# Five small changes of order in a fused encoder layer on one core: both ends, two recurrence heads, the attention's scores, and the first two loads of the output projection

## The chip, the cores and the metric

The kernel runs on one core of a Trainium2 chip. The metric is the device time of one execution in microseconds (us), as the median of several runs. Lower is better. Engine names are those of the profile: PE is TensorE (matmuls), PEld its weight loads, DVE is VectorE, ACT is ScalarE, POOL is GpSimd, SP is SyncE. SP issues nearly all loads; ACT and SP issue the stores.

## The reference

One encoder layer for 512 tokens of width 1024 in float32, cut to what matters:

```python
h = rms_norm(x, norm1_g)
proj = h @ w_in                       # pool, attention, recurrence inputs and three gates
y_pool = pool_mixer(u, pool_w, pool_scale)           # centred means over 2, 4, 8, 16 tokens
y_attn = diff_attention(aq, ak, av, lam, gain)       # 4 heads, two softmaxes each, ALiBi
y_rec  = hgrn2_mixer(rq, rf, rb, ri, rg, lb, gain)   # 4 heads, forward and backward scans
merged = g0 * (y_pool @ w_up_pool) + g1 * (y_attn @ w_up_attn) + g2 * (y_rec @ w_up_rec)
x = x + merged @ w_out
h2 = rms_norm(x, norm2_g)
gu = h2 @ w_ffn_in
x = x + (silu(gu[:, :2816]) * gu[:, 2816:]) @ w_ffn_out
return rms_norm(x, final_norm_g)
```

## The kernel before

**Matmuls.** Large products run as three float32r matmuls: both factors are split into a high part (a cast on ACT) and a low part (a subtraction on DVE), and hi·hi, lo·hi and hi·lo are summed in PSUM. For a weight these are `whi` (L185) and `wlo` (L186), for the normalised input `hT_hi` (L496) and `hT_lo` (L500). Small products of the recurrence and all transposes are plain float32 matmuls of 128x128.

**Weights.** A `Chunk` is one DMA of a weight (1 MB, or 512 KB) into a raw tile. By default the tile comes from the ring `wraw` of two buffers; a chunk with `where` takes it from a named pool (`LAST[where]`), which must have been opened. A `Part` is a piece of a chunk that is split into `whi` and `wlo`; three splits are held ahead. `Jobs.pump` emits loads in the order of the chunks: at most two live chunks of `wraw`, and a chunk with `where` as soon as its pool is there. Each engine works its own queue in order, so an instruction that waits holds all behind it on its engine. The orders of ACT, DVE and SP are set by a scheduler from its own simulated times (`issue_after` binds some of them), that of PE by the program.

**Order.** The layer runs in stages, and in each one several streams are woven together by `Pipe`: a planner with its own clock `t`, which each matmul advances by a fixed cost. A stream that yields `("w", c)` comes on again after `c` us of that clock; one that yields `("e", name, c)` comes on `c` us after the event `name`. The matmuls of `jobs.stream` fill what is between. PE's order of instructions is that of emission.

- At the start (L541 to about L600) four blocks of 128 rows of x are loaded. The gain row of the first norm is spread over 128 partitions by PE (`rc<-ident,g1c`) and copied to `g1b` in two halves by DVE (L577). `norm_rows` squares a block on ACT (L477), takes the reciprocal root on POOL (`ms` L148, then the power, L142), and multiplies on DVE in two halves (`hrow`, L483). `rows_T` transposes on PE (L98), and `hT_hi`, `hT_lo` follow. `probe` is filler for PE.
- `rec_scan(h)` is the stream of one recurrence head. After the event `V` it computes the states between blocks (`rc<-v_rec,kT`: two directions of three products, then `st` copies on ACT, L948, and the running sums on DVE, L951), waits 1.6 on the planner's clock and issues the outputs (`rc<-pt,v_rec` and `rc<-kq,st`). `kq,kc` are the products within a block, `pt` (L924) is their masked result. All share three PSUM banks named `rc`.
- `att_head(h)` is that of an attention head; it starts 6.0 after the event `AF{h}`, which stands behind the projection of keys. That evacuation makes k as hi parts and `l` as lo parts, the last of them by a copy on ACT (L1025). Scores are `rc<-k,q` and `rc<-l,q`. At a head's end the sums of squares go through PE (`tp<-fixed,sqo`), small DVE steps, a power on POOL (`rso`) and back through PE (`tp<-ident,rso`).
- The output projection: `quarter_parts(w_out[0], 0, 512, "wx")` gives two chunks of 256 columns, q0 and q1; `row_parts` gives two chunks for the other 512 columns, the row chunks, 1 MB each, whose splits go to a pool of their own. Beside them SP loads x again (2 MB) and `g2b`. Before the first quarter the last `up_job`s finish the merged tiles: for the tiles 4 to 7, DVE multiplies and adds (L758 to L762), ACT casts the hi part (L765, `y_arena<-gate`), DVE subtracts for the lo part (L766). `out_quarter_job` runs three blocks over k-tiles 0 to 5 first and then k-tiles 6 and 7.
- At the end `seven_job` finishes block after block of the final sum. `out_add` (L1410) adds PSUM to x; `out_sums` squares on ACT (L1417) and multiplies by the final gain on DVE (L1419); `out_rstd` sums on DVE and takes the power on POOL; `out_store(b)` scales 512 columns on ACT and 512 on DVE (L1441, L1443) and stores each half (256 KB) from ACT's and SP's queue. `behind` keeps what it holds after given instructions.

Of the kernel before, what the change touches and what calls it, by code (L numbers as in the profile page):

```python
# [14 lines left out]
AF = mybir.ActivationFunctionType  # L15
# [7 lines left out]
KT = D // P  # L23
# [15 lines left out]
class Pipe:  # L39
# [8 lines left out]
    def mark(self, name):  # L48
        self.events[name] = self.t
# [27 lines left out]
def encoder_kernel(ctx: ExitStack, tc: tile.TileContext, x, norm1_g, w_in, pool_w, pool_scale,  # L77
# [3 lines left out]
    nc = tc.nc  # L81
# [187 lines left out]
    @contextmanager  # L269
    def behind(after):  # L270

        with ExitStack() as st:
            for i in after:
                st.enter_context(tc.issue_after(i))
            yield
# [165 lines left out]
    def quarter_parts(w, c0, n, where=None, skip=0):  # L441

        v = w.rearrange("(kt p) c -> p kt c", p=P)
        for c in range(0, n, 256):
            ch = Chunk(v[:, :, c0 + c:c0 + c + 256], KT, 256, where if c == 0 else None)
            yield slice(c, c + 256), [Part(ch, lambda raw, j=j: raw[:, j:j + 4, :], 4, 256, None, skip)
                                       for j in (0, 4)]

# [78 lines left out]
    g_b = xg.tile([P, D], F32, name="g1b")  # L527
# [8 lines left out]
    for b in range(NB):  # L536
# [6 lines left out]
        if b >= 1:  # L543
            c = OFF[("rq", "rf", "rb")[b - 1]]
# [23 lines left out]
    gt = bank("tp")  # L568
# [4 lines left out]
    for half in range(2):  # L573
        gt = bank("rc", (P, 4, P))
        for j in range(4):
            transpose(gt[:, j, :], g_cols[:, half * 4 + j:half * 4 + j + 1].to_broadcast([P, P]), ident)
        nc.vector.tensor_copy(out=g_b[:, half * 512:half * 512 + 512], in_=gt.rearrange("p a b -> p (a b)"))  # L577

    probe = xg.tile([P, 1024], F32R, name="probe")
    nc.scalar.copy(out=probe, in_=ident.rearrange("p (o c) -> p o c", o=1).to_broadcast([P, 8, P]))  # L580
# [7 lines left out]
    first = []  # L588
# [10 lines left out]
    for b in range(2):  # L599
        where = ("tp", "rc")[b]  # L600
# [37 lines left out]
    for i in range(3):  # L638
        for n, _ in enumerate(cols_mm(ps0[i], first[i], hT, KT, 0, 0, 256, i == 0)):
            if (i, n) in ((1, 5), (2, 5)):  # L640
                b = 1 + i
# [227 lines left out]
    def rec_scan(h):  # L869
# [3 lines left out]
        kq, f, q = fronts[h]  # L873
# [26 lines left out]
        while n < P:  # L900
# [17 lines left out]
            a = strided(tot, toff, [[tstep, 2], [2, nb2]])  # L918
            c = strided(tot, toff + 1, [[tstep, 2], [2, nb2]])
# [9 lines left out]
        for d in range(2):  # L929
            ps = bank("rc", (P, NB, P))  # L930
            for j in range(3):
                b = j + d
# [1 line left out]
            nc.scalar.copy(out=kT[:, 3 * d:3 * d + 3, :], in_=ps[:, 0:3, :])  # L934
        mark(f"S{h}")
        yield ("e", "V", 0.8)
        yield ("w", 1.0)
        st = rh.tile([P, 6, P], F32, name="st", bufs=2)
        vs = [v_rec[:, b, h * P:(h + 1) * P] for b in range(NB)]
        for d in range(2):  # L940
# [4 lines left out]
            for prev, j in zip((None,) + order, order):  # L945
                own = st[:, 3 * d + j, :]
                if prev is None:
# [2 lines left out]
                total = strided(pyr, toff + d * S + j + d, [[1, 1]])  # L950
                nc.vector.scalar_tensor_tensor(out=own, in0=st[:, 3 * d + prev, :], scalar=total, in1=ps[:, j, :],  # L951
                                               op0=ALU.mult, op1=ALU.add)
        yield ("w", 1.6)
        ps = bank("rc")
        for b in range(NB):
            o = ps[:, b * P:(b + 1) * P]
# [77 lines left out]
    def att_head(h):  # L1034
        if h:
            yield ("e", f"QK{h - 1}", 0.0)
        if h > 1:
            yield ("e", f"AN{h - 2}", 0.0)
        yield ("e", f"AF{h}", 6.0)
        t = att.pop(h)  # L1040
        at, (vh, vl), aT, y_attn = ATT["at"], ATT["v"], ATT["aT"], ATT["y"]
        strip = ATT["strip"].tile([P, 896], F32, name="strip")
        nc.sync.dma_start(out=strip, in_=c_dist[h])
        zz = at.tile([P, NB, 2], F32, name="zz")
        rr = at.tile([P, NB], F32, name="rr")
        probs = {}

        def scores(i):
            bs = slice(i * P, (i + 1) * P)
            mx = small.tile([P, 2], F32, name="mx")  # L1050
            ex = []
            for c in range(2):
                ps = bank("rc")
                mm(ps, t[f"q{c}"][:, bs], t[f"k{c}"], True, False)
                mm(ps, t[f"q{c}"][:, bs], t[f"l{c}"], False, True)
                s = at.tile([P, S], F32, name=f"s{c}")

                nc.vector.tensor_tensor_reduce(out=s, in0=strip[:, 384 - P * i:896 - P * i], in1=ps, scale=1.0,  # L1058
                                               scalar=3.0e38, op0=ALU.add, op1=ALU.min, accum_out=mx[:, c:c + 1])
                nc.scalar.activation(out=s, in_=s, func=AF.Exp, scale=-1.0, bias=mx[:, c:c + 1],  # L1060
                                     accum_out=zz[:, i, c:c + 1])
                ex.append(s)

            co = small.tile([P, 2], F32, name="co")
            zn, co = co[:, 0:1], co[:, 1:2]
            nc.gpsimd.tensor_tensor(out=zn, in0=zz[:, i, 0:1], in1=nlam, op=ALU.mult)
            nc.gpsimd.tensor_tensor(out=co, in0=zz[:, i, 1:2], in1=minus1, op=ALU.pow)
            nc.gpsimd.tensor_tensor(out=co, in0=co, in1=zn, op=ALU.mult)
            nc.vector.scalar_tensor_tensor(out=ex[0], in0=ex[1], scalar=co, in1=ex[0], op0=ALU.mult, op1=ALU.add)
            probs[i] = ex[0]  # L1070

        def turn(i):
            bs = slice(i * P, (i + 1) * P)
            p = probs.pop(i)
            pt = bank("tp", (P, NB, P))
            for k in range(NB):
                transpose(pt[:, k, :], p[:, k * P:(k + 1) * P], ident)
            nc.scalar.copy(out=aT[0][:, :, bs], in_=pt)
            nc.vector.tensor_tensor(out=aT[1][:, :, bs], in0=pt, in1=aT[0][:, :, bs].bitcast(F32), op=ALU.subtract)

        scores(0)
        for i in range(NB):
            yield ("w", 1.6 + (0.7 if i == 0 else 0.0))
            if i + 1 < NB:
                scores(i + 1)
            else:
                mark(f"QK{h}")
            yield ("w", 2.4 + (1.0 if i + h == 0 else 0.0))
            if h and i == 0:
                yield ("e", f"PV{h - 1}", 0.0)  # L1090
            turn(i)
        mark(f"T{h}")
        nc.vector.reciprocal(out=rr, in_=zz[:, :, 0])
        yield ("e", "VA", 1.5)
        yield ("w", 1.5)
        ps = bank("rc")
        es = slice(h * P, (h + 1) * P)
        terms = [(vh, aT[0]), (vl, aT[0]), (vh, aT[1])]
        for i, (a, r) in enumerate(terms):
            for k in range(NB):  # L1100
                mm(ps, a[:, k, es], r[:, k, :], i == 0 and k == 0, i == 2 and k == NB - 1)
            yield
        mark(f"PV{h}")
        og, rbp = yield from head_norm(ps, at, gain_a, rr, 1)
        mark(f"AN{h}")
        nc.vector.tensor_tensor(out=og, in0=og, in1=rbp, op=ALU.mult)
        nc.scalar.copy(out=y_attn[0][:, h, :], in_=og)
        nc.vector.tensor_tensor(out=y_attn[1][:, h, :], in0=og, in1=y_attn[0][:, h, :].bitcast(F32),
                                op=ALU.subtract)
# [302 lines left out]
    def out_sums(b, c0, w, col, out_=None):  # L1412

        x = out_cols(b, c0, w)
        junk = FF["t"].tile([P, S], F32, name="silu")
        col = 4 * b + col
        sq = nc.scalar.activation(out=junk[:, 0:w], in_=x, func=AF.Square, scale=D ** -0.5,  # L1417
                                  accum_out=FF["stats"][:, col:col + 1]).ins
        nc.vector.tensor_tensor(out=x if out_ is None else out_, in0=x, in1=FF["g"][:, c0:c0 + w], op=ALU.mult)  # L1419
        return sq  # L1420
# [5 lines left out]
    def out_rstd(b, n):  # L1426

        st = [FF["stats"][:, 4 * b + i:4 * b + i + 1] for i in range(n)]
        ms = small.tile([P, 1], F32, name="ss2")
        if n == 2:  # L1430
            on_dve = nc.vector.tensor_tensor(out=ms, in0=st[0], in1=st[1], op=ALU.add).ins
        else:
            on_dve = nc.vector.scalar_tensor_tensor(out=ms, in0=st[1], scalar=st[0], in1=st[2],
                                                    op0=ALU.add, op1=ALU.add).ins
        rstd = small.tile([P, 1], F32, name="rstd")
        pow_mhalf(rstd, ms)
        return rstd, on_dve

    def out_store(b, rstd, src=None):
        a, c = out_cols(b, 512, 512), out_cols(b, 0, 512)  # L1440
        nc.scalar.activation(out=a, in_=a, func=AF.Copy, scale=rstd)  # L1441
        nc.scalar.dma_start(out=outb[b][:, 512:], in_=a)
        nc.vector.tensor_scalar(out=c, in0=c if src is None else src, scalar1=rstd, scalar2=None, op0=ALU.mult)  # L1443
        nc.sync.dma_start(out=outb[b][:, 0:512], in_=c)
# [157 lines left out]
    def seven_job():  # L1602
# [76 lines left out]
        late, _ = out_rstd(2, 2)  # L1679
        yield  # L1680
        own = bank("tp")
        src = FF["t"].tile([P, S], F32, name="u")
        first, second = slice(0, 256), slice(256, 512)
        sv_product(x[1][:, first], 7, 1, False, True, first)
        out_add(3, 256, x[1][:, second], ALU.subtract)
        out_add(3, 0, x[1][:, first], ALU.subtract)
        out_sums(3, 0, 256, 1, src[:, first])
        sv_product(own[:, second], 7, 1, True, True, second)
        out_add(3, 256, own[:, second], ALU.subtract)
        sq = out_sums(3, 256, 256, 2, src[:, second])  # L1690
        rstd, on_dve = out_rstd(3, 3)
        with behind((sq, on_dve)):
            out_store(2, late)
        out_store(3, rstd, src)
        yield

    for i, (j, _) in enumerate(PLAIN):
        ch = Chunk(wo[:, j:j + 2, :], 2, D)
# [136 lines left out]
```

## Time and profile before

| | us |
|---|---|
| median of 3 runs | 881.21 (880.99 to 881.6) |
| profiled execution | 880.92 |
| its span | 879.0 |
| PE busy | 866.3 (99%) |
| DVE busy | 660.8 (75%) |
| ACT busy | 448.9 (51%) |
| POOL busy | 37.8 (4%) |

The mean granted clock of TensorE is 0.998 of full speed, and the DMA engines moved 87.54 MB, at a mean of 100 GB/s. In a timeline each line is a start, a duration, an engine with its line, the operation with its output and inputs, and a count; in brackets stand the idle time before it and what ended it. "x3" lines are runs of like instructions. PE's matmuls overlap, so the duration of one is longer than the distance to the next.

### The profile page before, as it was taken

What the parts mean: (1) busy time and instruction counts of PE and PEld (TensorE: products, weight loads), DVE (VectorE), ACT (ScalarE), POOL (GpSimd) and SP (SyncE); (2) the same over time, 40 slices, a digit from 0 to 9 for tenths busy, and PEclk for the clock granted to TensorE, in tenths of its full rate; (3) what the DMA queues carried; (4) which work ended last, traced back from release to release, by engine and by line L of the source; (5) the groups of instructions that cost most, each with busy time, mean ns of one, the idle gap of its engine ahead of it and who ended that gap; (6) DMA issues with size and microseconds to landing.
All of it is one profiled execution on the core that took longest, in us unless ns stands there. A gap on an engine that the chain in (4) does not pass through costs nothing.

```text
span 879.0 us, 14111 instructions
## 1 busy us (share of the span) xinstructions
PE 866.3 (99%) x5713; PEld 786.4 (89%) x5713; DVE 660.8 (75%) x978; ACT 448.9 (51%) x718; POOL 37.8 (4%) x83
## 2 busy tenths in 40 slices
PE   8999999999999999999999999999999999999996
PEld 7989988888997888899999898999999999988885
DVE  6788655854757787987876645997888888847996
ACT  6544333525747764563355335755655655533563
POOL 2000000000112230000000001000000000000001
PEclk9999999999999999999999999999999999999999
DMA  8330113124133131343331770253433433355002
GB/s 244 97 120 25 50 48 96 48 73 138 45 96 94 52 104 48 97 134 107 96 97 48 263 192 1 54 139 106 135 97 98 137 102 98 120 192 191 1 1 97
DMA packets 115694, 87.54 MB, mean 100 GB/s; under 512 B 3862, under 2 KB 104748, under 8 KB 115628
## 3 DMA queue, kind: packets, MB, share of 16 engines
q1 hardware_dynamic: 115036, 85.57, 32.2%
q8 instruction: 45, 0.74, 0.4%
q10 hardware_dynamic: 592, 1.05, 0.3%
q14 instruction: 21, 0.17, 0.1%
HBM read 84.52 MB, written 2.10 MB: 99 GB/s over the span
## 4 chain that ended last, share of the span: by engine, by line
PE 86%; issue 7%; DVE 3%; DMA 2%; ACT 1%; POOL 1%; POOLq 0%; DVEq 0%; ACTq 0%
PE mm L90 56%; PE rc L90 26%; PE tp L90 2%; PE tp L98 2%; DMA raw<-in_w_out_dram 1%; DVE wlo L186 1%; DVE hrow L483 1%; DMA raw<-in_w_in_dram 0%; ACT whi L185 0%; DVE hT_lo L500 0%; PE rc L98 0%; ACT s L1060 0%; POOL rso L142 0%; DVE g1b L577 0%; ACT l L1025 0%
## 5 line engine op out<-in xcount | busy, mean ns | idle before, releaser
L185 ACT CAST whi<-raw 128x1024 fp32r<-128x1024 f32 (+1 forms) x134 | 127.6, 958 | 141.5 <-PE mm L90 90.7
L186 DVE TENSOR_TENSOR wlo<-raw,whi 128x1024 fp32r<-128x1024 f32 (+1 forms) x134 | 147.5, 1106 | 51.2 <-ACT whi L185 35.4
L90 PE MATMUL mm<-hT_hi,whi 128*128 128x512 f32 (+1 forms) x344 | 82.4, 371 | 0.0
L90 PE MATMUL mm<-hT_hi,wlo 128*128 128x512 f32 (+1 forms) x344 | 81.4, 370 | 0.2 <-DVE wlo L186 0.2
L90 PE MATMUL mm<-hT_lo,whi 128*128 128x512 f32 (+1 forms) x344 | 81.1, 369 | 0.0
L304 DVE TENSOR_TENSOR slo<-sums,shi 128x1024 fp32r<-128x1024 f32 x58 | 70.6, 1218 | 0.3 <-ACT shi L302 0.3
L90 PEld LDWEIGHTS mm<-hT_hi,whi 128*128 128x128 f32 x344 | 59.0, 189 | 9.8 <-ACT hT_hi L496 0.4
L90 PEld LDWEIGHTS mm<-hT_lo,whi 128*128 128x128 f32 x344 | 59.1, 189 | 9.5
L90 PEld LDWEIGHTS mm<-hT_hi,wlo 128*128 128x128 f32 x344 | 58.7, 189 | 9.6 <-DVE wlo L186 0.4
L302 ACT CAST shi<-sums 128x1024 fp32r<-128x1024 f32 x58 | 61.0, 1052 | 4.6 <-DVE sums L266 3.7
L263 DVE TENSOR_TENSOR sums<-raw 128x1024 f32<-128x1024 f32 x29 | 35.4, 1219 | 1.5 <-DMA raw<-in_w_in_dram 1.5
L90 PE MATMUL mm<-y_arena,whi 128*128 128x512 f32 x128 | 32.5, 394 | 0.0
L90 PE MATMUL mm<-whi,y_arena 128*128 128x256 f32 (+1 forms) x192 | 31.9, 316 | 0.2 <-ACT whi L185 0.2
L916 DVE TENSOR_TENSOR kq<-kq,pyr 128x256 f32<-128x256 f32 x48 | 18.2, 421 | 18.1 <-PE rc L90 18.0
L90 PE MATMUL rc<-kq,kc 128*128 128x128 f32 x224 | 31.6, 285 | 0.0
L90 PEld LDWEIGHTS rc<-kq,kc 128*128 128x128 f32 x224 | 30.1, 191 | 1.5
L90 PEld LDWEIGHTS mm<-whi,y_arena 128*128 128x128 f32 x192 | 27.4, 188 | 3.2 <-ACT whi L185 0.8
L885 ACT COPY kc<-kq 128x512 f32<-128x512 f32 x28 | 18.6, 666 | 20.4 <-PE rc L90 12.7
L1060 ACT ACTIVATE s<-s,mx 128x512 f32<-128x512 f32 x32 | 23.1, 721 | 10.9 <-DVE mx L1058 10.7
L90 PEld LDWEIGHTS mm<-y_arena,whi 128*128 128x128 f32 x128 | 23.8, 188 | 5.0
L1350 DVE TENSOR_TENSOR g<-mm,g 128x256 f32<-128x256 f32 x21 | 8.9, 424 | 23.7 <-PE mm L90 23.7
L90 PE MATMUL mm<-fhi,slo 128*128 128x256 f32 x168 | 26.1, 278 | 0.6 <-DVE slo L304 0.5
(386 smaller groups left out, 2045.7 us busy)
## 6 DMA issues: line engine op xcount, KB each, us to landing
raw<-in_w_in_dram SPq DMA_DIRECT2D x44, 512.0 KB, 4.1
raw<-in_w_ffn_in_dram SPq DMA_DIRECT2D x44, 512.0 KB, 5.3
raw<-in_w_in_dram SPq DMA_DIRECT2D x8, 1024.0 KB, 5.2
raw<-in_w_ffn_out_dram SPq DMA_DIRECT2D x7, 1024.0 KB, 4.9
raw<-in_w_out_dram SPq DMA_DIRECT2D x4, 1024.0 KB, 11.1
xin<-in_x_dram SPq DMA_DIRECT2D x4, 512.0 KB, 4.6
raw<-in_w_up_rec_dram SPq DMA_DIRECT2D x2, 1024.0 KB, 6.6
raw<-in_w_up_pool_dram SPq DMA_DIRECT2D x2, 1024.0 KB, 5.1
```

Source lines behind the costliest of these rows:

```text
L90: i = nc.tensor.matmul(out_, lhsT=lhsT, rhs=rhs, start=start, stop=stop, skip_group_check=chain)
L98: tc.keep_in_program_order(nc.tensor.transpose(out_, in_, idn))
L185: nc.scalar.copy(out=hi, in_=view)
L186: LAST["wlo"] = nc.vector.tensor_tensor(out=lo, in0=view, in1=hi.bitcast(F32), op=ALU.subtract).ins
L263: nc.vector.tensor_tensor(out=strided(sums, 0, [[2 * half, 2], [1, half]]), in0=strided(self.raw, 0, [[3 * half, 2], [1, half]]), in1=stri ...
L302: nc.scalar.copy(out=hi, in_=view)
L304: on_dve = nc.vector.tensor_tensor(out=lo, in0=view, in1=hi.bitcast(F32), op=ALU.subtract).ins
L483: on_dve = nc.vector.scalar_tensor_tensor(out=h[:, cs], in0=src[:, cs], scalar=rstd, in1=g_b[:, cs], op0=ALU.mult, op1=ALU.mult).ins
L885: nc.scalar.copy(out=strided(kc, 0, [[2 * n, S // (2 * n)], [n, 2], [1, n]]), in_=strided(kq, 2 * S, [[2 * n, S // (2 * n)], [S + n, 2], [ ...
L916: nc.vector.tensor_tensor(out=xv, in0=xv, in1=tv, op=ALU.mult)
L1060: nc.scalar.activation(out=s, in_=s, func=AF.Exp, scale=-1.0, bias=mx[:, c:c + 1], accum_out=zz[:, i, c:c + 1])
L1350: on_dve = nc.vector.tensor_tensor(out=c["g"], in0=c["x"], in1=c["g"], op=ALU.add).ins
```

## The change

There are five edits. (1) Of the two quarter chunks of w_out, the second now goes to the pool `wx`, the first to the ring `wraw`. (2) The second half of the gain row is copied by ACT. (3) Head 1's states come 4.5 and not 1.0 after `V` plus 0.8, and the outputs of heads 0 and 1 come 2.4 after the states and not 1.6. (4) Heads 2 and 3 of the attention start 7.0 after `AF`. (5) The store of block 2 is emitted behind the sums of the first half of block 3, and no longer behind the last sums.

```diff
-            ch = Chunk(v[:, :, c0 + c:c0 + c + 256], KT, 256, where if c == 0 else None)
+            ch = Chunk(v[:, :, c0 + c:c0 + c + 256], KT, 256, where if c else None)
...
-        nc.vector.tensor_copy(out=g_b[:, half * 512:half * 512 + 512], in_=gt.rearrange("p a b -> p (a b)"))
+        (nc.scalar.copy if half else nc.vector.tensor_copy)(
+            out=g_b[:, half * 512:half * 512 + 512], in_=gt.rearrange("p a b -> p (a b)"))
...
-        yield ("w", 1.0)
+        yield ("w", 4.5 if h == 1 else 1.0)
...
-        yield ("w", 1.6)
+        yield ("w", 2.4 if h < 2 else 1.6)
...
-        yield ("e", f"AF{h}", 6.0)
+        yield ("e", f"AF{h}", 7.0 if h > 1 else 6.0)
...
-        out_sums(3, 0, 256, 1, src[:, first])
+        with behind((out_sums(3, 0, 256, 1, src[:, first]),)):
+            out_store(2, late)
...
-        sq = out_sums(3, 256, 256, 2, src[:, second])
-        rstd, on_dve = out_rstd(3, 3)
-        with behind((sq, on_dve)):
-            out_store(2, late)
-        out_store(3, rstd, src)
+        out_sums(3, 256, 256, 2, src[:, second])
+        out_store(3, out_rstd(3, 3)[0], src)
```

In the changed kernel the lines from L578 to L1686 have numbers one higher, those behind L1694 one lower.

PE in the recurrence, heads 0 and 1, before. `rc<-v_rec,kT` are the state products, `rc<-pt,v_rec` and `rc<-kq,st` the outputs, `mm<-hT_hi,whi` a projection:

```order
L90 MATMUL mm<-hT_hi,whi 128x512 x6
L90 MATMUL rc<-kq,kc 128x128 x4
L90 MATMUL rc<-v_rec,kT 128x128 x12
L90 MATMUL mm<-hT_hi,whi 128x512 x2
L90 MATMUL rc<-pt,v_rec 128x128
L90 MATMUL rc<-kq,st 128x128
L90 MATMUL rc<-pt,v_rec 128x128
L90 MATMUL rc<-kq,st 128x128 x2
```

The same place now:

```order
L90 MATMUL mm<-hT_hi,whi 128x512 x6
L90 MATMUL rc<-kq,kc 128x128 x4
L90 MATMUL rc<-v_rec,kT 128x128 x6
L90 MATMUL mm<-hT_hi,whi 128x512 x2
L90 MATMUL mm<-hT_lo,whi 128x512 x6
L90 MATMUL rc<-kq,kc 128x128 x4
L90 MATMUL rc<-pt,v_rec 128x128
L90 MATMUL rc<-kq,st 128x128
```

Head 1's six state products have gone from here; they stand behind the outputs of head 0, and eight projection matmuls and four `kq,kc` stand between head 0's states and its outputs.

ACT around the output projection, before. `whi<-raw` are the casts of weights, `y_arena<-gate` those of the merged tiles 4, 5, 6 and 7:

```order
L716 ACTIVATE gate<-mm 128x256
L765 CAST y_arena<-gate 128x512 x2
L185 CAST whi<-raw 128x1024 x2
L765 CAST y_arena<-gate 128x512
L185 CAST whi<-raw 128x1024
L765 CAST y_arena<-gate 128x512
L185 CAST whi<-raw 128x1024 x8
```

The same place now:

```order
L185 CAST whi<-raw 128x1024
L717 ACTIVATE gate<-mm 128x256
L766 CAST y_arena<-gate 128x512
L185 CAST whi<-raw 128x1024
L766 CAST y_arena<-gate 128x512 x2
L185 CAST whi<-raw 128x1024 x3
L766 CAST y_arena<-gate 128x512
L185 CAST whi<-raw 128x1024 x6
```

The casts of q0's two parts stand earlier, ahead of merged tiles 4 and 5. Three casts stand between tiles 6 and 7: q1's first part and both of the first row chunk. Of the six behind tile 7 the first two are the second row chunk's, the third is q1's second part; before, that part stood ahead of the second row chunk.

SP in the same stretch, before and now in one piece of the difference; `raw<-in_w_out_dram` are the chunks of w_out (8x256 a quarter, 4x512 a row chunk), `x` is the input that is loaded again:

```order
-L1753 DMA x_4903<-in_x_dram 128x4x1024
-L164 DMA raw<-in_w_out_dram 128x8x256 x2
+L164 DMA raw<-in_w_out_dram 128x8x256
+L1752 DMA x_4905<-in_x_dram 128x4x1024
+L164 DMA raw<-in_w_out_dram 128x8x256
 L164 DMA raw<-in_w_out_dram 128x4x512
```

One quarter chunk, q0, has moved ahead of x; q1 and the first row chunk stay behind it, in this order.

## The prediction

> **What bounds the kernel now.** I read the busy times first, then the waits of TensorE, then the timeline around each place that the change touches.
>
> ```profile
> PE 866.3 (99%) x5713; PEld 786.4 (89%) x5713; DVE 660.8 (75%) x978; ACT 448.9 (51%) x718; POOL 37.8 (4%) x83
> ...
> PE rc L90 <- ACT l L1025: 0.8, 1, 0.8
> PE tp L98 <- DVE hrow L483: 0.7, 1, 0.7
> PE mm L90 <- DVE wlo L186: 0.6, 2, 0.4
> PE rc L90 <- DVE pt L924: 0.5, 1, 0.5
> ...
> PE rc L90 <- ACT st L948: 0.4, 1, 0.4
> PE tp L98 <- POOL rso L142: 0.3, 1, 0.3
> ```
>
> The first line is the page's: TensorE (PE) is busy for 99% of the span. The others are its waits (total, number, longest): each is short and happens once or twice, and each delays everything behind it, because no later idle time on PE absorbs it. So a removed PE wait shows in the time at full size, and so does a new one. Only the stores behind PE's last matmul are another bound. The change removes no work and adds none; the question is which waits go and which come. The profiled execution took 880.92 us: span 879.0 and 1.92 around it, 0.29 under the median of 881.21. I sum against 880.92 and add 0.29 at the end. Below about 0.2% (1.76 us) a measurement of this kernel can't tell a change from none.
>
> **Start: the gain row's second half copied by ACT.**
>
> ```profile
> 5.68 0.19 POOL L148 TENSOR_SCALAR ms<-ss 128x1 f32<-128x1 f32 x1 [1.02 <-ACT hrow L477]
> ...
> 6.84 0.75 DVE L483 SCALAR_TENSOR_TENSOR hrow<-xin,rstd,g1b 128x512 f32<-128x512 f32 x1
> 7.02 0.62 POOL L148 TENSOR_SCALAR ms<-ss 128x1 f32<-128x1 f32 x1 [0.51 <-ACT hrow L477]
> ...
> 7.51 1.05 ACT L185 CAST whi<-raw 128x1024 fp32r<-128x1024 f32 x1 [0.57 <-DMA raw<-in_w_in_dram]
> 7.51 0.68 DVE L577 COPY g1b<-rc 128x512 f32<-128x512 f32 x1
> ...
> 7.73 0.55 POOL L142 TENSOR_TENSOR rstd<-ms,mhalf 128x1 f32<-128x1 f32 x1
> 8.23 2.08 DVE L483 SCALAR_TENSOR_TENSOR hrow<-xin,rstd,g1b 128x512 f32<-128x512 f32 x3
> 8.46 0.58 ACT L496 CAST hT_hi<-tp 128x512 fp32r<-128x512 f32 x1
> ...
> 9.04 0.65 PE L98 MATMUL tp<-ident,hrow 128*128 128x128 f32 x4 [0.73 <-DVE hrow L483]
> ```
>
> PE waits 0.73 at 9.04 for block 0's second hrow, which stands on VectorE (DVE) behind the copy at 7.51. ACT waits for a DMA until 7.51 (0.57 of idle time); its own read of a 512-column bank took 0.58 (8.46), so the copy fits there, from 6.94 to 7.52, and delays whi by nothing to speak of. That hrow then starts at about 7.6, up to 0.65 earlier. But POOL's power for block 1 (7.73, 0.55) ran beside the copy, which reads PSUM; now it runs beside an hrow that reads xin and g1b from SBUF. The pair at 6.84 and 7.02 shows the price: the POOL step that took 0.19 at 5.68 took 0.62 beside an hrow and ended with it. Held in this way, the power ends about 0.4 after that hrow, at 8.65, and block 1's two hrow run until about 10.05, against 10.31 now: 0.25 gained, not 0.65. The Trainium skill's "SBUF — State Buffer", section "Who interferes with whom", speaks against this edit in the same way: a DVE instruction with two SBUF inputs and a GpSimd one that reads SBUF fully block each other; by that rule, too, the larger gain is lost, and the row at 7.02 agrees with it. Later waits of the start hang on the same chain and move with it. I take −0.25, with ends −0.65 (no hold) and 0 (the next wait absorbs it).
>
> **Recurrence: second head's states later.**
>
> ```profile
> 117.16 0.74 PEld L90 LDWEIGHTS rc<-v_rec,kT 128*128 128x128 f32 x6 [0.67 <-PE rc L90]
> ...
> 118.50 0.75 PEld L90 LDWEIGHTS rc<-v_rec,kT 128*128 128x128 f32 x6 [0.60 <-ACT st L948]
> ```
>
> Heads 0 and 1 now put all four state products back to back. The rc banks of the third and fourth are still being read, hence 0.67 and 0.60 of waiting. In the new order only head 0's six and six are adjacent in PE's row of 12 to 6, then eight projection matmuls and four kq,kc stand before head 0's outputs, and head 1's six come behind those outputs. Both waits go: −1.27. What is late next is the last state of each head: followed through banks, ACT's copies and DVE's scan by the durations of this trace, I find the states ready about 0.3 before PE's outputs ask for them, and nothing else late. I take −1.2. The ends are −1.4 (the cheaper switches between small and large matmuls) and 0, where as much waiting returns at the later products.
>
> **Attention: head 2's and 3's first scores a little later.**
>
> ```profile
> 278.51 0.62 ACT L1025 CAST l<-l 64x512 fp32r<-64x512 f32 x1
> ...
> 279.15 0.59 ACT L1078 CAST aT_hi<-tp 128x512 fp32r<-128x512 f32 x1
> ...
> 279.18 0.50 PE L90 MATMUL rc<-l,q 128*128 128x512 f32 x1 [0.81 <-ACT l L1025]
> ...
> 337.83 1.02 POOL L142 TENSOR_TENSOR rso<-mo,mhalf 128x4 f32<-128x4 f32 x1 [9.94 <-DVE mo L667]
> 338.02 2.00 PE L90 MATMUL mm<-hT_hi,wlo 128*128 128x512 f32 x8
> ...
> 339.86 0.60 PE L98 MATMUL tp<-ident,rso 128*128 128x128 f32 x4
> ```
>
> The last lo score of head 2 asks for l at about 278.2 and gets it at 279.13, so PE stands still for close to 1 us (0.81 in the row and the pipeline's refill). Six projection matmuls now come first; by 339.86 − 338.02 for eight, one is 0.23, six are 1.38, and the score is due at about 279.6, after l. That cover was work which stood behind the scores; the product of aT_hi now follows them at once, at 279.8, and aT_hi is ready at 279.74: up to 0.1 lost. At the end of attention the same shift leaves eight matmuls (1.84), not twelve, between the last sqo sums and the rso transposes, while the chain of small steps with POOL's 1.02 takes about 2.1: 0.2 to 0.3 of new waiting. Net −0.7, with ends −1.0 and 0.
>
> **Output projection: the first two weight loads trade buffers.**
>
> ```profile
> 470.40 0.69 DVE L186 TENSOR_TENSOR wlo<-raw,whi 128x512 fp32r<-128x512 f32 x1 [0.54 <-ACT whi L185]
> ...
> ...
> 486.51 6.51 SPq L164 DMA_DIRECT2D raw<-in_w_out_dram  x3
> ...
> 496.20 2.00 ACT L185 CAST whi<-raw 128x1024 fp32r<-128x1024 f32 x2 [2.15 <-DMA raw<-in_w_out_dram]
> ...
> 498.25 0.99 PEld L90 LDWEIGHTS mm<-whi,y_arena 128*128 128x128 f32 x8 [0.42 <-ACT whi L185]
> ...
> 499.21 1.05 ACT L185 CAST whi<-raw 128x1024 fp32r<-128x1024 f32 x1 [0.49 <-DMA raw<-in_w_out_dram]
> ...
> 500.29 0.30 PEld L90 LDWEIGHTS mm<-wlo,y_arena 128*128 128x128 f32 x2 [0.59 <-DVE wlo L186]
> ...
> 506.77 1.98 PE L90 MATMUL mm<-whi,y_arena 128*128 128x256 f32 x16
> ...
> 508.38 1.05 ACT L185 CAST whi<-raw 128x1024 fp32r<-128x1024 f32 x1 [4.33 <-PE mm L90]
> 508.58 1.07 PE L90 MATMUL mm<-wlo,y_arena 128*128 128x256 f32 x8
> ...
> GB/s 0 0 23 70 222 386 392 410 404 427 415 380 379 360 345 351 348 350 347 350 366 389 389 404 398 322 35 0 0 0 0 0 41 178 413 401 401 88 0 27
> ```
>
> Now 2 MB of x go ahead of the first chunk of w_out, which lands at 496.2, and PE waits 0.42 and 0.59 for its parts. With the ordinary ring the first chunk needs only a raw buffer whose last reader, the wlo at 470.40, is done at 471.1, so SP issues it ahead of x, and its 1 MB is there long before 496. Both waits go: −0.95 with the restarts.
>
> The edit adds a wait of another kind. ACT's cast of the last merged tile (L765, as L766 in the changed kernel) now stands behind three whi, the last two of them from the first row chunk of w_out, so it can't run until that chunk has landed. PE needs it late: by 508.58 − 506.77 for 16, one of these matmuls is 0.113, and 54 of them (three blocks, three terms, six k-tiles) lie between 497.3 and the first use, which gives 503.4 for the hi part and about 503.8 for the lo part. From the landing, two whi (2.0 in the row at 496.20), the cast (0.6) and DVE's lo parts behind them need about 4.4. So the landing decides from 499.1 on, and PE then loses 1 us for each us. The last line is the DMA traffic from 484 to 512 in slices of 0.7: it falls to 35 at 502.2, after g2b, whose 0.5 MB at 400 GB/s take 1.3, in part beside the row chunk; so I put the chunk's landing between 501 and 501.5 today. With one chunk of 1 MB less ahead of it (2.7 us at 390 GB/s) that becomes 498.3 to 498.8: 0.3 to 0.8 of margin. Behind that cast ACT has the second row chunk's two casts and then q1's second part, which its buffer holds back until about 507.4 anyway (508.38 today, where PE's last matmuls of q0 release it, less the 0.95); that row chunk lands by about 502.7, so nothing is lost there. I take −0.8. The ends are −0.95 and, with a landing at 501.5 as today, 2.4 − 0.85 = +1.55.
>
> **End: the third block's store moves up.**
>
> ```profile
> 870.23 0.55 POOL L142 TENSOR_TENSOR rstd<-ss,mhalf 128x1 f32<-128x1 f32 x1 [6.41 <-DVE ss L1431]
> ...
> 873.55 0.72 POOL L142 TENSOR_TENSOR rstd<-ss,mhalf 128x1 f32<-128x1 f32 x1 [2.77 <-DVE ss L1433]
> ...
> 873.90 1.26 SPq L1444 DMA_DIRECT2D out_dram<-x  x2
> ...
> 875.06 0.34 ACTq L1442 DMA_DIRECT2D out_dram<-x  x1
> ...
> 876.00:877.00 1.00, 0.00 (x0) 0.00 (x0) 0.00 (x0) 0.00 (x0) 0.00 (x0) 0.60 0.99 381
> 877.00:878.00 1.00, 0.00 (x0) 0.00 (x0) 0.00 (x0) 0.00 (x0) 0.00 (x0) 0.50 0.52 191
> ```
>
> The windows end with the DMA share and GB/s: four stores of 256 KB keep the DMA engines full until about 877.5. Block 2's two stores now leave at 871.4 and 872.2, while PE still works, and only 512 KB remain. With the scaling at 873.39 gone from beside it, the last power should take 0.55, not 0.72, so the last stores are issued by 874.65 and 874.9; at 381 GB/s the 1.05 MB that end at 877.5 began at about 874.75, 0.9 after the issues at 873.9, so data now begin at about 875.55, and 0.52 MB take 1.38: 876.9. I take −0.65. The ends are −0.8 and −0.15, where only the power's 0.17 remains, because a lone store may be held by its own latency. By the Trainium skill's "DMA: Bandwidth & Descriptors", section "Specifications", most of a DMA's cost is a fixed completion of about 2 us; the end would then follow the last issue alone and the gain would be 0.5 smaller. The full share from 876 to 877 speaks against it: there the engines are busy with data, not waiting. ACT's block 2 scaling ends at about 872.1 and its DMA issue at 872.5, 0.2 before its next square at 872.71: no loss there.
>
> **Sum.** 0.25 + 1.2 + 0.7 + 0.8 + 0.65 = 3.6: 880.92 − 3.6 = 877.3, and with 0.29, **877.6 us** at the median; its own range is 876.5 to 878.7.
>
> **Rivals.** First, the waits in the middle move and don't go: recurrence and attention give nothing. For it: the margins there are 0.3 and less. Against it: PE has other work between. 877.6 + 1.9 = 879.5, chance 0.13. Second, the row chunk lands as late as today, ACT's cast holds PE: 877.6 + 2.35 = 879.95, chance 0.10. Third, by the fixed cost of a store the tail gives 0.15 only: 878.1, chance 0.07. Fourth, on the slower side: the same cast waits for a landing that is later than today's, because the transfers of x, two w_out chunks, g2b and the next row chunk (5.5 MB from 486.2) share the engines, and move at 290 GB/s, under the 345 of the slowest full slice above. The first row chunk then lands with the last at 505.2, PE loses 505.2 − 499.1 = 6.1, and the time is 877.6 + 0.8 − 0.85 + 6.1 = 883.65; it decides for slower (over 882.97) from a landing at 504.5 on. Chance 0.04, since SP issues them one behind the other. The forecast keeps 0.66.
>
> **Numbers.** Faster by over 0.2% means under 879.45: the forecast, the third rival and half of the first, 0.79. Slower is the fourth, 0.04; the rest, 0.17, is the same. The range leaves out the second and the fourth rival at the top, and the forecast's lowest part: 876.4 to 879.6.
>
> **What would show it.** Right: no PE wait at 9.04 over 0.4, none over 0.2 in 116 to 136 or at 279, none for whi or wlo at 497 to 501, 0.2 to 0.3 at the last rso, and behind SP's last issue the traffic of two stores only, about 1.4 us of it. Wrong: a PE wait for y_arena at 503, behind ACT's whi; new waits of 0.5 and more for st; last stores that take as long as before. A time above 879.5 would refute the sum.

## The result, and the profile after

The changed kernel takes **877.81 us** (median of 6 runs, 876.91 to 878.32), the kernel before 881.4 (6 runs, 880.99 to 881.74): a ratio of 0.9961, 95% interval 0.9951 to 0.9971. So it is faster by 3.6 us, as forecast (877.6); the terms behind the sum came out less evenly than the sum. The profiled execution of the changed kernel, with a span of 876.5, is the slowest of its six (878.32), and the reason is part of what follows. Of the 19 runs of the kernel before whose median, 881.33, is used further down, one was slow (1764.94); no ratio counts it, and without it the median is 881.23.

The waits of TensorE (PE) in the changed kernel, as before in total, number and longest; a wait for ident at the very start (1.3) and one for hT_lo (0.2), which both kernels have, stand beside these:

```profile
PE rc L98 <- DVE hrow L483: 0.5, 1, 0.5
PE mm L90 <- DVE slo L304: 0.4, 1, 0.4
PE rc L90 <- DVE st L952: 0.3, 1, 0.3
PE tp L98 <- POOL rso L142: 0.3, 1, 0.3
PE mm L90 <- DVE wlo L186: 0.2, 1, 0.2
```

The waits for l, pt, st of ACT, whi, and one for wlo are gone. A wait for hrow is still there, at another block; a wait for st from DVE is new. (The wait for rso was there before; it is one of the recurrence, at 200 us.)

**A ledger.** Since PE works nearly without a pause, the start of one and the same PE instruction in two traces shows what was gained up to it. Here is one of the output projection in the timeline before (shown above at 506.77) and now:

```profile
503.87 2.05 PE L90 MATMUL mm<-whi,y_arena 128*128 128x256 f32 x16
...
505.75 1.11 PE L90 MATMUL mm<-wlo,y_arena 128*128 128x256 f32 x8
```

503.87 − 506.77 = −2.90. The differences of such shifts give each stage its part. All kernels below are measured in this way, each against the one profiled execution before; minus is gained, in us:

| kernel | to 24 us (start) | to 200 (recurrence) | to 380 (attention) | to 507 (first half of w_out) | to 530 | to 600 | behind PE | span |
|---|---|---|---|---|---|---|---|---|
| changed | −0.10 | −0.92 | −0.82 | −1.06 | +0.54 | +0.58 | −0.70 | −2.48 |
| only_wout | +0.06 | +0.01 | +0.03 | −1.06 | +0.54 | −0.01 | −0.01 | −0.44 |
| only_rec | +0.11 | −0.90 | +0.15 | −0.15 | 0 | 0 | −0.01 | −0.80 |
| only_att | −0.38 | −0.01 | −0.57 | −0.02 | 0 | +0.58 | 0 | −0.40 |
| only_end | +0.08 | −0.02 | +0.05 | −0.03 | 0 | +0.08 | −0.71 | −0.55 |
| only_start | −0.64 | 0 | +0.18 | +0.66 | 0 | +0.58 | −0.02 | +0.77 |
| gain_psum | −0.70 | −0.90 | −0.84 | −1.07 | +0.54 | −0.01 | −0.71 | −3.69 |
| late_rows | +0.27 | −0.91 | −1.04 | −0.88 | 0 | −0.02 | −0.77 | −3.35 |
| psum_late | −0.42 | −0.89 | −0.87 | −0.58 | 0 | +0.07 | −0.76 | −3.45 |
| mid_wide | −0.14 | −0.90 | −0.95 | −0.83 | +0.56 | +1.10 | −0.70 | −1.86 |
| psum_small | +0.39 | −0.89 | −0.88 | −1.00 | 0 | +1.31 | −0.71 | −1.78 |

(Behind 600 nothing differs up to PE's last product. A span here is one execution, so a kernel's median need not follow it. How far a stage scatters is seen in the kernels whose edits leave it alone: by up to 0.02 in the recurrence, from +0.03 to +0.18 in the attention, from −0.15 to +0.66 up to 507.)

### The profile page after: what moved, and what is told of

It is laid out like the page before. It is cut to its first block, busy times and chain, and to the rows that moved or that the text cites. A ratio compares the mean times of both kernels' runs of the same rounds, so it can differ in the third digit from the quotient of the medians.

```text
span 876.5 us, 14112 instructions
## 1 busy us (share of the span) xinstructions
PE 866.8 (99%) x5713; PEld 788.1 (90%) x5713; DVE 659.1 (75%) x977; ACT 448.7 (51%) x719; POOL 35.8 (4%) x83
```

## The experiments

**Each edit alone.** The edits are those of the diff above.

Only the trade of buffers (`where if c else None`):

> Only the trade of buffers of the first two w_out loads, the rest as before. My theory: both PE waits of 498 and 500 go (0.95), no new PE wait appears at the last merged tile, and the 256-column matmuls of the output projection then keep the slower pitch that the changed kernel showed there (0.118 and not 0.113 us, 192 matmuls: 0.9 given back by 520 us), because no stall breaks their rhythm; the total comes out between -0.1 and -0.5 us. Rival: the slower pitch in the changed kernel was chance and has nothing to do with this edit; then the pitch here is 0.113 and the total is -0.9 to -1.0 us.

Measured: 880.5 us against 881.59, ratio 0.9989 (0.9980 to 0.9998). The timeline of its output projection:

```profile
505.80 2.05 PE L90 MATMUL mm<-whi,y_arena 128*128 128x256 f32 x16
507.69 1.11 PE L90 MATMUL mm<-wlo,y_arena 128*128 128x256 f32 x8
```

Sixteen products take 1.89, 0.118 each, where the kernel before needs 1.81 (0.113). Both waits are gone (−1.06 by 507) and 0.54 is given back by 530, as in the changed kernel. So the slower pitch comes with this edit; the rival is out. The median gained 1.1, more than the trace's 0.44: one execution isn't the median (the profiled one before, 880.92, lies 0.67 under the 881.59), and what the others did isn't shown.

Only the recurrence (`4.5 if h == 1 else 1.0`, `2.4 if h < 2 else 1.6`):

> Only the recurrence's two delays. My theory: the waits of 0.67 and 0.60 at the state products go and one of 0.3 to 0.5 for the last state of head 1 comes in their place near 136 us: -0.9 us. Rival: that new wait comes from the other edits ahead of it (the start is 0.1 earlier in the changed kernel); then it is absent here and the total is -1.2 to -1.3 us.

Measured: 880.53 against 881.59, ratio 0.9989 (0.9980 to 0.9998). Its timeline near 136:

```profile
135.44 0.68 DVE L968 TENSOR_TENSOR og<-og,tp 128x512 f32<-128x512 f32 x1
...
136.04 0.34 DVE L951 SCALAR_TENSOR_TENSOR st<-st,pyr,rc 128x128 f32<-128x128 f32 x1
...
136.43 0.30 PEld L90 LDWEIGHTS rc<-kq,st 128*128 128x128 f32 x2 [0.50 <-DVE st L951]
```

The new wait is here too, 0.50 on the weight load, and the stage gives −0.90. It belongs to the edit and not to what runs ahead of it. But the state that is late is head 2's, not head 1's as the text above says: it belongs to the third group of state products, and the section on the prediction shows it in the changed kernel.

Only the attention (`7.0 if h > 1 else 6.0`):

> Only the attention's delay of 7.0 for heads 2 and 3. My theory: the wait for l at 279 goes and at most 0.1 to 0.2 comes at the last rso transposes: -0.85 us. Rival, from the prediction: the rso chain costs 0.25 and the product of aT_hi 0.05: -0.7 us.

Measured: 880.45 against 881.59, ratio 0.9985 (0.9977 to 0.9994). The timeline around 279:

```profile
278.97 0.59 ACT L1078 CAST aT_hi<-tp 128x512 fp32r<-128x512 f32 x1
278.98 0.40 PE L90 MATMUL rc<-k,q 128*128 128x512 f32 x1
279.21 0.39 PE L90 MATMUL rc<-l,q 128*128 128x512 f32 x1
279.61 0.76 PEld L90 LDWEIGHTS rc<-aT_hi,va_hi 128*128 128x128 f32 x4 [0.43 <-ACT aT_hi L1078]
```

No score waits any more. The product of aT_hi does: it would have followed at 279.44 (0.23 behind the score at 279.21) and came at 279.61, 0.17 lost. The stage gives −0.57; in the six kernels with all edits it gives −0.82 to −1.04. The expectation's two values lie between, so the totals don't tell them apart. The rows at the last rso transposes do: they start 2.18 behind the first of the eight products ahead of them (336.69 to 338.87), where eight need 1.93 by the rate of the trace before, so 0.25 is lost there, which is the price that the rival puts on it.

Only the end:

> Only the earlier store of block 2. My theory: the last two stores alone take about 1.4 us of traffic where four took 2.75, and the last power takes 0.55 and not 0.72: -0.65 to -0.75 us. Rival, the fixed cost of a store: what ends the kernel is the last store's own latency, so only the earlier issue counts: -0.15 to -0.25 us.

Measured: 881.01 against 881.59, ratio 0.9989 (0.9981 to 0.9998). Its windows, with DMA share and GB/s at the end:

```profile
874.00:875.00 1.00, 0.00 (x0) 0.00 (x0) 0.48 (x1) 0.72 (x1) 0.20 (x1) 1.00 0.00 0
875.00:876.00 1.00, 0.00 (x0) 0.00 (x0) 0.00 (x0) 0.00 (x0) 0.00 (x0) 1.00 0.40 152
876.00:877.00 1.00, 0.00 (x0) 0.00 (x0) 0.00 (x0) 0.00 (x0) 0.00 (x0) 0.99 0.96 371
877.00:878.00 1.00, 0.00 (x0) 0.00 (x0) 0.00 (x0) 0.00 (x0) 0.00 (x0) 0.50 0.01 2
```

Only 525 KB are left, and data end at 877.0 (877.5 before, although PE is 0.16 later here). The tail is 0.71 shorter. By PE's progress the last store is issued 0.24 earlier (874.98 − 0.16 against 875.06), which is all that the rival allows; the other 0.47 come from the amount of data, not from the last store's own latency.

Only the start (`(nc.scalar.copy if half else nc.vector.tensor_copy)`):

> Only the copy of the gain row's second half on ACT. My theory: POOL's power for block 1 takes about 0.95 beside the hrow that reads two operands from SBUF and ends with it, so PE's wait moves from 9.04 to the next block's transposes, and the sum of the two waits falls by 0.1 to 0.25 us only. Rival (no blocking between POOL and DVE; the power keeps its 0.55): 0.5 to 0.65 us less.

Measured: 880.97 against 881.33, ratio 0.9995 (0.9986 to 1.0004), no difference that can be told; its runs lie in two groups, at 879.8 to 880.0 and 880.7 to 881.6. The profiled one gained 0.64 at the start, against the theory. Its timeline says why:

```profile
7.54 0.56 POOL L142 TENSOR_TENSOR rstd<-ms,mhalf 128x1 f32<-128x1 f32 x1
7.59 2.08 DVE L483 SCALAR_TENSOR_TENSOR hrow<-xin,rstd,g1b 128x512 f32<-128x512 f32 x3 [0.18 <-ACT g1b L577]
```

Here the power began 0.05 ahead of the hrow; it kept 0.56, and the three hrow kept 0.69 each. In the changed kernel it began behind:

```profile
6.93 1.41 DVE L483 SCALAR_TENSOR_TENSOR hrow<-xin,rstd,g1b 128x512 f32<-128x512 f32 x2
...
7.81 0.94 POOL L142 TENSOR_TENSOR rstd<-ms,mhalf 128x1 f32<-128x1 f32 x1
...
8.79 1.42 DVE L483 SCALAR_TENSOR_TENSOR hrow<-xin,rstd,g1b 128x512 f32<-128x512 f32 x2 [0.45 <-POOL rstd L142]
...
9.60 1.38 PE L98 MATMUL rc<-ident,hrow 128*128 128x128 f32 x8 [0.53 <-DVE hrow L483]
```

The hrow that it met ends at 8.34, and the power 0.41 later. Which of the two comes first depends on when the first gain copy runs, and that comes in two ways, with the edit and without: at 5.4 to 5.7 us in 4 of the 12 traces (3 of 7 with the edit and 1 of 5 without, only_att, which is 0.38 earlier) and at 6.0 to 6.3 in the others. What differs is TensorE's clock: by the clock records of the traces full speed begins at 4.4 to 5.1 us in these four and at 5.8 to 7.6 in the other eight, and PE's eight transposes ahead of the copy (`rc<-ident,g1c`) take 1.04 to 1.09 in the four and 1.33 to 1.92 in the eight. Like against like, the edit gives −0.26 in the early way (only_start against only_att); in the late way −0.10 in the changed kernel and −0.14 in mid_wide. The +0.27 of late_rows, late too, is mostly not the edit's: at 16 us that trace is at +0.03, and the rest comes from a wait for hT_lo at 20 us (0.41, against 0.18 before). The power took 0.94 in all three of these. In only_start the 0.46 that PE was ahead before w_out was lost there, with 0.2 more: the first chunk landed no earlier (its first whi at 496.41), and PE waited for it longer.

**Does the second SBUF input hold POOL?** The changed kernel, with block 0's second hrow reading the gain from its PSUM bank:

```diff
+        LAST["gt"] = gt.rearrange("p a b -> p (a b)")
...
+            g = LAST.pop("gt") if half and "gt" in LAST else g_b[:, cs]
-            on_dve = nc.vector.scalar_tensor_tensor(out=h[:, cs], in0=src[:, cs], scalar=rstd, in1=g_b[:, cs],
+            on_dve = nc.vector.scalar_tensor_tensor(out=h[:, cs], in0=src[:, cs], scalar=rstd, in1=g,
```

> The changed kernel, but block 0's second hrow takes the gain from the PSUM bank and not from g1b, so that it reads one operand from SBUF, not two. If two SBUF inputs are what holds POOL: the power for block 1 runs beside it in 0.55, block 1's hrow start by 8.45 and not 8.79, and PE's wait of 0.5 at 9.6 shrinks by about 0.35; total -0.35 us against the changed kernel. If any DVE operation held POOL, or if it was the power's own time: the power takes 0.9 as before and nothing is gained (0).

Measured: 877.42 (877.12 to 878.15) against 881.33, ratio 0.9958 (0.9946 to 0.9971). The start gave −0.70, but this was the early way again, with the power 0.01 ahead of the hrow, so the question stayed open. psum_late (below) came in the late way:

```profile
7.57 0.75 DVE L484 SCALAR_TENSOR_TENSOR hrow<-xin,rstd,rc 128x512 f32<-128x512 f32 x1
7.78 0.56 POOL L142 TENSOR_TENSOR rstd<-ms,mhalf 128x1 f32<-128x1 f32 x1
8.37 1.41 DVE L484 SCALAR_TENSOR_TENSOR hrow<-xin,rstd,g1b 128x512 f32<-128x512 f32 x2
```

The power starts while that hrow runs, and takes 0.56, not 0.94; block 1's hrow start at 8.37, not 8.79, and the start gives −0.42, not −0.10. So the operand that DVE reads from SBUF beside xin is what holds POOL. The Trainium skill's "SBUF — State Buffer", section "Who interferes with whom", has this rule, and both cases agree with it. That page of the Trainium skill also says that the one that starts first keeps the other out for its whole instruction; in only_start DVE, 0.05 behind POOL, lost nothing, so in this one case that half isn't borne out.

**Does the last merged tile hang on the row chunk's landing?** The changed kernel, with a copy of 512 KB from x to the output in DRAM (overwritten at the end) queued behind x:

```diff
-    nc.sync.dma_start(out=LAST["x2"], in_=x2d.rearrange("(b p) d -> p b d", p=P))
+    loaded = nc.sync.dma_start(out=LAST["x2"], in_=x2d.rearrange("(b p) d -> p b d", p=P)).ins
+    with tc.issue_after(loaded):
+        nc.sync.dma_start(out=outb[0], in_=xblk[0])
```

> The changed kernel with a copy of 512 KB from x to the output in DRAM (overwritten later) queued behind x, ahead of q1 and the first row chunk; the order on ACT is unchanged. It delays the row chunk's landing by 1.3 us (by the 390 GB/s of this stretch) to 2.6 us (if reading and writing DRAM count twice). My theory, the second rival of the prediction: the cast of the last merged tile waits for that landing, the margin is 0.4 to 0.7, and beyond it PE waits 1 us for each us: +0.6 to +2.2 us, as a new PE wait for y_arena near 501 to 504. Rival: the landing has slack enough, or the cast isn't held: 0, no new PE wait.

Measured: 877.78 (877.0 to 878.14) against 881.33, ratio 0.9961 (0.9947 to 0.9974). First the changed kernel, then this one:

```profile
497.23 2.00 ACT L185 CAST whi<-raw 128x1024 fp32r<-128x1024 f32 x2 [1.34 <-DMA raw<-in_w_out_dram]
...
499.13 0.61 ACT L766 CAST y_arena<-gate 128x512 fp32r<-128x512 f32 x1
...
500.58 0.69 DVE L767 TENSOR_TENSOR y_arena<-gate,y_arena 128x512 fp32r<-128x512 f32 x1
...
501.75 0.63 PE L90 MATMUL mm<-whi,y_arena 128*128 128x256 f32 x4
```

```profile
498.29 2.00 ACT L185 CAST whi<-raw 128x1024 fp32r<-128x1024 f32 x2 [1.59 <-DMA raw<-in_w_out_dram]
...
501.65 0.68 DVE L767 TENSOR_TENSOR y_arena<-gate,y_arena 128x512 fp32r<-128x512 f32 x1
...
502.38 0.19 PEld L90 LDWEIGHTS mm<-whi,y_arena 128*128 128x128 f32 x1 [0.17 <-DVE y_arena L767]
...
504.21 1.98 PE L90 MATMUL mm<-whi,y_arena 128*128 128x256 f32 x16
...
506.02 1.07 PE L90 MATMUL mm<-wlo,y_arena 128*128 128x256 f32 x8
```

In the changed kernel the lo part is ready at 501.27, 0.7 before PE needs it (about 501.98). Here the landing is 0.9 later by PE's own progress (498.29 + 1.68 against 497.23 + 1.84, the shifts at 497 added), and PE waits 0.17. In psum_late it is 1.2 later (498.08 + 2.18) and the wait is 0.46. So the hold is real, its margin is 0.7, and beyond it PE loses about 1 us per us.

The surprise is in the last two rows: behind the wait sixteen products take 1.81 again, 0.113 each. The 0.17 that was lost saved 0.54 by 530.

**What ends the slow pitch?** The changed kernel with one product that nothing reads, behind the first 18 of the projection: of 512 columns in mid_wide,

```diff
+                if b == 0:
+                    mm(bank("tp"), m[0][:, 0, 0:P], m[0][:, 0, :], True, True)
```

and of 128 columns in float32 in psum_small, which takes the gain from PSUM too:

```diff
+                if b == 0:
+                    mm(bank("tp")[:, 0:P], ident, ident, True, True)
```

> The changed kernel with one 512-column product that nothing reads (0.23 us of PE) behind the first 18 products of the output projection. If the slower pitch of the 256-column products there is a rhythm that a disturbance ends: the pitch falls from 0.118 to 0.113 behind it, 174 products gain 0.8, net -0.55 us against the changed kernel. If the pitch comes from what runs beside (DMA traffic, other engines' accesses): it stays 0.118, net +0.23 us.

> The changed kernel with block 0's second hrow taking the gain from PSUM, and with one float32 128x128 product that nothing reads (0.11 us and a switch of 0.09) behind the first 18 products of the output projection. Two questions. The pitch: if any break in the 256-column products ends the slow rhythm, the pitch falls from 0.118 to 0.113 behind it and 0.5 us are gained net; if only a wait of PE does (a 512-column product did not), it stays at 0.118 and 0.2 us are lost. POOL: if two SBUF inputs are what holds it, the power for block 1 takes 0.55 also where it starts while the second hrow is running (0.94 in the changed kernel); if any DVE operation does, about 0.9.

Measured: mid_wide 879.12 (878.01 to 879.7) against 881.33, ratio 0.9974 (0.9964 to 0.9984); psum_small 878.7 (877.66 to 879.25) against 881.28, ratio 0.9967 (0.9955 to 0.9980). The first row is mid_wide's, the second psum_small's, each at the same place:

```profile
506.77 2.05 PE L90 MATMUL mm<-whi,y_arena 128*128 128x256 f32 x16
```

```profile
507.11 1.98 PE L90 MATMUL mm<-whi,y_arena 128*128 128x256 f32 x16
```

Sixteen in 2.05 is the slow pitch, in 1.98 the other. The wide product changed nothing; the small one ended the slow pitch, and psum_small gives back none of its −1.00. Both kernels are slower than the changed one all the same: in both PE waits near 568 for a weight of the next stage (shi, 1.2 and 1.4), which none of the ten other traces shows. Its cast stands on ACT behind another cast, and that one waits for a weight to land; this is mid_wide's row, and the changed kernel has the same cast at 564.29 without such a wait:

```profile
566.05 1.06 ACT L185 CAST whi<-raw 128x1024 fp32r<-128x1024 f32 x1 [2.05 <-DMA raw<-in_w_ffn_in_dram]
```

In the DMA records of these two traces that weight's packets start over 5.6 and 5.8 us, in the ten others over 4.0 to 4.3. And in these two a fetch of instructions (16 KB, 1.0 us) starts in the middle of them, at 563.3 and 563.4; in the others it starts as they end. So an added instruction that moves a fetch fits both, but no run tests it. (psum_small also lost 1.3 to a wait for hT_lo at the start, which stands in its +0.39.)

Whether a short wait does it again:

> The changed kernel with the gain from PSUM for block 0's second hrow, and with the 512 KB copy from x to the output in DRAM ahead of q1 and the first row chunk. If a short wait of PE ends the slow rhythm, as one of 0.17 us seemed to do in the run with the copy alone: such a wait shows again near 502, the pitch behind it is 0.113, and the output projection is 0.4 to 0.6 us shorter than in the changed kernel. If that was chance: the pitch stays at 0.118 and the wait adds 0.2. POOL as in the run beside it.

Measured: 877.63 (876.95 to 878.55) against 881.28, ratio 0.9958 (0.9945 to 0.9972). The wait of 0.46 came, and the pitch behind it is 0.113. But the wait was longer, so the stage ends at −0.58, little better than the −0.52 of the changed kernel by 530. The expected 0.4 to 0.6 was not had. Against the changed kernel's 877.81, neither this nor gain_psum can be told apart by these runs.

## Why the prediction came out right, point by point

- **Start, −0.25.** The mechanism is shown: POOL's power took 0.94 and ended 0.4 behind the hrow, as worked out. The size was −0.10 in the profiled execution, because hrow of block 1 started at 8.79 and not at 8.65, and it depends on an order that changes from one execution to the next, with the moment at which PE comes to full speed.
- **Recurrence, −1.2.** It is −0.92. The two waits went, and heads 0 and 1 have their last state 0.8 and 1.1 before its first use (118.55 against 119.35, 124.56 against 125.63 in the changed kernel), more than the 0.3 forecast. The step that failed is "nothing else late": head 2, whose delays the edit leaves as they were, comes earlier too. Its state products, the third group behind 115.07 and 121.36, start at 132.36 and not at 138.05:

```profile
132.36 1.50 PE L90 MATMUL rc<-v_rec,kT 128*128 128x128 f32 x12
...
134.10 0.68 DVE L968 TENSOR_TENSOR og<-og,sg 128x512 f32<-128x512 f32 x1
...
135.23 0.68 DVE L969 TENSOR_TENSOR og<-og,tp 128x512 f32<-128x512 f32 x1
...
135.82 0.34 DVE L952 SCALAR_TENSOR_TENSOR st<-st,pyr,rc 128x128 f32<-128x128 f32 x1
...
136.21 0.30 PEld L90 LDWEIGHTS rc<-kq,st 128*128 128x128 f32 x2 [0.50 <-DVE st L952]
```

There its last state stands on DVE behind two steps of head 1's normalisation (L968, L969), and PE waits 0.31 for it. New waiting at the later products was one end of the range; it came at a quarter of that price.
- **Attention, −0.7.** It is −0.82, and in its parts too. The wait at 279 went. The new waiting of 0.2 to 0.3 for rso came, though the list of PE's waits doesn't show it:

```profile
335.80 2.09 PE L90 MATMUL mm<-hT_hi,wlo 128*128 128x512 f32 x8
...
337.66 0.16 DVE L670 TENSOR_TENSOR rso<-rso,rr 128x4 f32<-128x4 f32 x1 [1.13 <-POOL rso L142]
...
337.97 0.62 PE L98 MATMUL tp<-ident,rso 128*128 128x128 f32 x4
```

The transposes come 2.17 behind the start of these eight products. Before, twelve took 2.85 (337.01 to 339.86), so eight, with four times 0.23 less, need 1.93: about 0.25 is lost. The term for the product of aT_hi (up to 0.1) was not needed in the changed kernel (0.24 behind the last score, no wait); in only_att it cost 0.17.
- **Output projection, −0.8.** Both waits went and no wait came behind the row chunk: −1.06 by 507, better than forecast. The margin of 0.7 lies in the forecast's 0.3 to 0.8 partly by luck: by the clock of the trace before the chunk is there at 499.07 (497.23 + 1.84), later than the 498.3 to 498.8 forecast and at the very point from which PE was to lose time, but the chain behind it takes 4.0 and not 4.4. And the term took the pitch of 0.113 from the trace before as a property of these products. It is the pitch behind a wait, and by 530 the stage is at −0.52.
- **End, −0.65.** It is −0.70, and in its parts too: the power took 0.55 (first row below), the last issue came at 873.04 (874.82 on the clock of the trace before, forecast 874.9), and the amount of data set the end, as only_end shows. The rival of the fixed cost is out. (In the Trainium skill's "DMA: Bandwidth & Descriptors" the 2 us stand in the section "Anatomy of one DMA — SWDGE (gpsimd) path", as a fit for DMAs that GpSimd issues; these stores are issued by ACT and SP.)

```profile
871.71 0.55 POOL L142 TENSOR_TENSOR rstd<-ss,mhalf 128x1 f32<-128x1 f32 x1 [2.72 <-DVE ss L1434]
...
873.04 0.34 ACTq L1443 DMA_DIRECT2D out_dram<-x  x1
```

- **The sum.** The five terms add up to −3.06 in the trace, against −3.6. The profiled execution shows only −2.48, because of 0.58 at a place that no edit touches (572 to 590 us), and it is the slowest of its six. The medians differ by 3.6, so 0.5 of the agreement has no term behind it: start, recurrence and output projection were put 0.15, 0.28 and 0.28 too high, attention and end only 0.12 and 0.05 too low, while the one execution before that all terms are measured against lies 0.48 under its median of 881.4. Every term has the right sign; that the number came within about 0.2 us is partly luck. The rival in which the waits of the middle only move is out: recurrence and attention gave 1.74 of the 1.9.

## What to carry to other kernels

Where the bounding engine has no idle time, compare the start of the same instruction in two traces, stage by stage: that gives an edit its price to about 0.05 us where the stage repeats (here recurrence and end), and to a few tenths where it hangs on landings or on single waits, while run times of one edit alone scatter by 1 us. A stream that moves takes those behind it along, so look for new waits in the streams that were not edited too. A wait of 0.25 can be missing from the list of waits; count the products between two starts. Ask of each duration that a sum is built on what stood before it in the trace, because a pitch measured behind a stall need not hold once the stall is gone. A cast that shares its queue with work gated by a DMA is as late as that DMA; work out the landing that it can bear before moving loads.

## What the hardware showed that was not expected

Products of 128x256 run at two pitches, at the same granted clock (1.00 in the windows from 490 to 520 us of both kernels): 0.113 and 0.118 us, and a run keeps the one that it has. In the output projection the five traces with PE's waits for whi and wlo have 0.113 behind them; the four without a wait (changed, only_wout, gain_psum, mid_wide) keep 0.118 over 192 products; late_rows and psum_late change at their wait, psum_small at its float32 product. The second place is behind the wait for slo at 572, which all twelve traces have. Here are the kernel before and the changed kernel, each with two rows of the same products:

```profile
574.53 0.74 PE L90 MATMUL mm<-fhi,slo 128*128 128x256 f32 x4 [0.48 <-DVE slo L304]
...
588.71 0.62 PE L90 MATMUL rc<-h_hi,whi 128*128 128x256 f32 x4
```

```profile
572.16 0.74 PE L90 MATMUL mm<-fhi,slo 128*128 128x256 f32 x4 [0.38 <-DVE slo L304]
...
586.87 0.63 PE L90 MATMUL rc<-h_hi,whi 128*128 128x256 f32 x4
```

The same products take 14.18 before and 14.71 now. Three of the twelve (changed, only_att, only_start) are slow here and nine fast, whatever their edits. Ahead of this wait five are slow (changed, only_end, only_start, gain_psum, mid_wide): three of them turn fast at it, and only_att turns slow. So behind a wait, either pitch may follow. What selects it stays open; a wait or a float32 product can end the slow one, and a 512-column product did not.
